# A masked softmax on one core: two whole loads move from SyncE's DMA queue to GpSimd's, ahead of the narrow loads

## The chip, the core and the metric

The kernel runs on one core of one Trainium2 chip. The metric is the device time in microseconds (us) of one execution; of the kernel before there are three, with a median of 155.32 us (155.14 to 155.57).

## The reference

The input is `x`, 16 batches x 8 heads x 256 rows x 256 columns in float32, and a length for each batch. In this draw the lengths lie between 157 and 252. Each row is a softmax over its first `length` columns; the columns behind are zero.

```python
for b in range(batch):
    length = lengths[b]
    masked = x[b, :, :, :length].copy()
    masked = masked - np.max(masked, axis=-1, keepdims=True)
    exp_masked = np.exp(masked)
    result[b, :, :, :length] = exp_masked / np.sum(exp_masked, axis=-1, keepdims=True)
```

## The kernel before

**Tiles.** One batch is one tile: 2,048 rows, 16 for each of 128 partitions, 256 columns, 2.1 MB. The buffer `xt` has eight slots for tiles; every step works in place. Tiles are taken in the order of `batch_of`: positions 0, 1 and 2 are batches 1, 2 and 3, position 3 is batch 0, and from position 4 on the position is the batch. In this text "tile 2" and "load 2" mean position 2.

**Loads.** The first three tiles are loaded whole, since they are fetched before the lengths are known. Tile 0 comes in two halves (L136), tiles 1 and 2 in one DMA each (L138), all issued by SyncE (SP), so they stand one behind the other in SP's queue, which the profile calls q1. From position 3 on GpSimd (POOL) issues *narrow* loads (`pick`, L158) through its own queue, q0: it reads the length into a register, walks through a tree of branches to the nearest width that is not smaller, and loads only so many columns of each row. (For lengths over the widest step it loads the whole tile.) The columns that such loads leave out are zeroed once for slots 3 to 7 (`fill`, L181).

**Compute, per tile.** VectorE (DVE) applies the mask (`clip`, L240: columns behind the length become hugely negative), ScalarE (ACT) does the exponential of 16 rows per partition and their sums in two halves (L347), and DVE takes reciprocals (L261) and multiplies (`divide`, L264), again in two halves. DVE's order is written out: the masks of tile 0's two halves, the divide of its first half, the mask of tile 1, the divide of its second half, then the mask of tile 2, both divides of tile 1, and from then on first divide, next mask, second divide.

**Stores.** SP issues them (L147) in two or three parts for most tiles, each after the divide that it needs (`s_out`). Ahead of all stores stands one wait for three masks (`s_min`, 3): both halves of tile 0 and tile 1. So stores share q1 with the first three loads, and come behind them.

**What orders POOL.** POOL makes constants (L171 to L177), waits for two early DVE steps, fills slot 3, and waits for the lengths, for its fill, and for the second half of tile 0 (`s_ld[1]`). Then come narrow load 3, the fills of slots 4 to 7, a wait for them and one for two divides (`s_out`, 2), and a loop (L193) for the remaining loads, in which load n waits until load n-2 has landed and the stores of the tile that had its slot are done:

```python
fill(ahead)
nc.gpsimd.wait_ge(s_word, 16)
nc.gpsimd.wait_ge(s_fill, 1)
nc.gpsimd.wait_ge(s_ld[1], 16)
v_len = length(POOL, word[0:1, 0:1])
pick(v_len, 0, ahead, 1, [160, 176, 192, 208, 224, seq_k])
for b in range(ahead + 1, slots):
    fill(b)
nc.gpsimd.wait_ge(s_fill, slots - ahead)
nc.gpsimd.wait_ge(s_out, 2)
```

At the end a check of all sums decides whether a slow exact path runs; it does not run with this data.

Of the kernel before, what the change touches and what calls it, by code (L numbers as in the profile page):

```python
# [21 lines left out]
def kernel(  # L22
# [6 lines left out]
    nc = tc.nc  # L29
# [9 lines left out]
    x_f = x.rearrange("b h q k -> b (h q) k").rearrange("b (p t) k -> b p t k", p=P)  # L39
# [5 lines left out]
    ahead = 3  # L45
    assert ahead == 3 and slots == 8 and batch == 16

    def batch_of(pos):
        return pos + 1 if pos < ahead else 0 if pos == ahead else pos
# [22 lines left out]
    xt = pool.tile([P, slots, nt, seq_k], F32, name="xt")  # L72
# [26 lines left out]
    with tc.tile_critical(no_gpsimd_drain=True):  # L99
# [4 lines left out]
        s_ld = [sem(f"s_ld{k}") for k in range(ahead + 1)]  # L104
# [8 lines left out]
        s_out = sem("s_out")  # L113
# [10 lines left out]
        def length(engine, at):  # L124

            return nc.values_load(
                at,
                engines=[engine],
                skip_runtime_bounds_check_because="compared with constants, never an address",
            )  # L130
# [3 lines left out]
        for h in range(2):  # L134
            s = slice(h * half, (h + 1) * half)
            nc.sync.dma_start(out=xt[:, 0, s], in_=x_f[batch_of(0), :, s]).then_inc(s_ld[h], 16)  # L136
        for b in range(1, ahead):
            nc.sync.dma_start(out=xt[:, b], in_=x_f[batch_of(b)]).then_inc(s_ld[b + 1], 16)  # L138

        nc.sync.wait_ge(s_min, 3)  # L140
        for b in range(batch):
            s_b = s_st[b % 2]
            for s in parts(b):
                nc.sync.wait_ge(s_out, 2 * b + (s.stop - 1) // half + 1)
                if b >= 2 and s.start == 0:
                    nc.sync.wait_ge(s_b, 64 * (b // 2 + 1))
                nc.sync.dma_start(  # L147
                    out=out_f[batch_of(b), :, s, :], in_=xt[:, b % slots, s, :]
# [26 lines left out]
        nc.gpsimd.memset(ones_c, 1.0).then_inc(s_ones, 1)  # L175
        for par in range(2):
            nc.gpsimd.memset(seed[:, par : par + 1], 0.0).then_inc(s_st[par], 64)  # L177
        nc.gpsimd.wait_ge(s_v, 2)

        def fill(b):  # L180
# [2 lines left out]
        fill(ahead)  # L183
        nc.gpsimd.wait_ge(s_word, 16)
        nc.gpsimd.wait_ge(s_fill, 1)
        nc.gpsimd.wait_ge(s_ld[1], 16)
        v_len = length(POOL, word[0:1, 0:1])
        pick(v_len, 0, ahead, 1, [160, 176, 192, 208, 224, seq_k])
        for b in range(ahead + 1, slots):
            fill(b)  # L190
        nc.gpsimd.wait_ge(s_fill, slots - ahead)
        nc.gpsimd.wait_ge(s_out, 2)
        with nc.Fori(0, batch // 2 - 2, 1, engines=[POOL]) as q:  # L193
            for par in range(2):
                n = 2 * q + (ahead + 1 + par)
# [19 lines left out]
        def step(ins):  # L215
# [8 lines left out]
                out=down, in0=iota_i, scalar1=0.5, scalar2=-big, op0=ALU.add, op1=ALU.mult  # L224
# [7 lines left out]
                out=len_s, in0=len_f, scalar1=big, scalar2=None, op0=ALU.mult  # L232
# [65 lines left out]
        for k, (_, _, edge, op) in enumerate(checks):  # L298
            nc.vector.tensor_scalar(  # L299
                out=bad[:, k : k + 1],  # L300
# [13 lines left out]
        with nc.vector.Else():  # L314
            with nc.Fori(0, batch, 1, engines=[DVE]) as i:
                nc.vector.wait_ge(g_ld, 16 * i + 16)
                nc.vector.scalar_tensor_tensor(
                    out=g_t,
# [8 lines left out]
                    out=neg_max, in_=g_t, op=ALU.max, axis=AX, negate=True  # L327
# [5 lines left out]
                    out=g_t,  # L333
# [25 lines left out]
        with nc.scalar.If(a_redo >= 1):  # L359
            for par in range(2):  # L360
                nc.scalar.wait_ge(s_st[par], 64 * (batch // 2 + 1))
            with nc.Fori(0, batch, 1, engines=[ACT]) as i:
                nc.scalar.dma_start(out=g_t, in_=x_g[:, bass.ds(i, 1)]).then_inc(g_ld, 16)
                nc.scalar.wait_ge(g_v, 3 * i + 2)
                with nc.Fori(0, nt, 1, engines=[ACT]) as t:
                    e = g_t[:, bass.ds(t, 1), :]
                    nc.scalar.activation(
                        out=e,
                        in_=e,
# [41 lines left out]
```

## Time and profile before

| | before |
|---|---|
| median of three executions | 155.32 us |
| the profiled execution | 155.53 us |
| its span, first to last instruction | 153.9 us |
| DVE busy | 116.9 us, 76% |
| ACT busy | 105.4 us, 68% |
| POOL busy | 21.6 us, 14% |
| bytes moved | 61.57 MB (read 27.98, written 33.55), mean 400 GB/s |

The profile is one execution. Its page gives busy time for each engine, then the span in 40 equal slices of 3.85 us; in the row of DMA each digit is the busy share of the 16 DMA engines in tenths, and the row below has what they moved. Queues are named by number: q1 is SP's, q0 is POOL's. Further views list an engine's instructions in order of time (start, duration, engine, line, operation, and in brackets the idle time before and what ended it), the chain of waits back from the last instruction, and busy time and GB/s in windows of one's choice. A DMA's landing is the time when its completion is seen; the trace also has a record of every DMA packet, with its queue, size and start. All times count from the start of the span.

### The profile page before, as it was taken

The numbers are of one execution on the slowest core, as the hardware profiler recorded it, in microseconds if no ns is written. First come the engines' busy times: TensorE is split into PE (matmuls) and PEld (weight loads), VectorE is DVE, ScalarE is ACT, GpSimd is POOL, SyncE is SP. The second block draws the span as 40 slices with busy tenths as digits, with TensorE's granted clock in tenths as the row PEclk, the third lists the DMA queues.
The fourth block names the chain that finished last, engine by engine and source line by source line (L and its number), as shares of the span: only waits on it lengthen the run. The fifth ranks groups of instructions, "written<-read, shape, count | busy, mean of one in ns | idle before, by whom it ended". The sixth has DMA issues, their size and how long they took to land.

```text
span 153.9 us, 1306 instructions
## 1 busy us (share of the span) xinstructions
PE 0.3 (0%) x2; PEld 0.2 (0%) x2; DVE 116.9 (76%) x91; ACT 105.4 (68%) x514; POOL 21.6 (14%) x28
## 2 busy tenths in 40 slices
PE   0000000000000000000000000000000000000000
PEld 0000000000000000000000000000000000000000
DVE  1359779997969696969889696969697676968700
ACT  3096899569595959597795959595968819597000
POOL 4139320100220200202030020211010000000000
DMA  4999999999999999999999999999999999999992
GB/s 124 428 445 419 319 376 418 414 409 442 416 404 387 423 411 420 409 414 415 400 421 411 413 411 404 411 420 415 418 416 421 424 441 417 430 449 413 432 422 119
DMA packets 10357, 61.57 MB, mean 400 GB/s; under 512 B 866, under 2 KB 978, under 8 KB 6642
## 3 DMA queue, kind: packets, MB, share of 16 engines
q1 hardware_dynamic: 5904, 39.85, 63.0%
q0 software_dynamic: 4448, 21.69, 35.2%
q14 instruction: 3, 0.02, 0.0%
q10 hardware_dynamic: 2, 0.00, 0.0%
HBM read 27.98 MB, written 33.55 MB: 400 GB/s over the span
## 4 chain that ended last, share of the span: by engine, by line
DMA 44%; DVE 29%; ACT 10%; issue 7%; ACTq 3%; SPq 1%; POOLq 0%; PE 0%
DMA xt<-in_x_dram 25%; DMA out_dram<-xt 19%; DVE xt L264 15%; DVE xt L240 12%; ACT xt L347 10%; ACTq L347 3%; DVE inv_sum L261 1%; SPq L136 1%; DVE ends L296 0%; SPq L147 0%; ACTq L353 0%; SPq L138 0%; DVE bad L299 0%; PE count L210 0%; POOLq L163 0%
## 5 line engine op out<-in xcount | busy, mean ns | idle before, releaser
L347 ACT ACTIVATE xt<-xt (+1 forms) x256 | 102.4, 402 | 34.3 <-DVE xt L240 34.3
L264 DVE TENSOR_TENSOR xt<-xt,inv_sum 128x2048 f32<-128x2048 f32 x32 | 73.3, 2292 | 1.1
L347 ACT ACTIVATION_READ_ACCUMULATOR xt<-xt (+1 forms) x256 | 48.0, 187 | 0.0
L240 DVE SCALAR_TENSOR_TENSOR xt<-down,len_s,xt 128x2048 f32<-128x2048 f32 (+1 forms) x17 | 37.8, 2221 | 8.2 <-DMA xt<-in_x_dram 8.1
L158 POOL DMA_DIRECT2D xt<-in_x_dram x13 | 13.9, 1073 | 90.4 <-DMA out_dram<-xt 60.1
L261 DVE RECIPROCAL inv_sum<-row_sum 128x8 f32<-128x8 f32 x32 | 6.4, 199 | 16.6 <-ACT xt L347 16.6
L181 POOL MEMSET xt<- 128x1536 f32 x5 | 6.7, 1400 | 1.1 <-DVE len_s L231 1.1
L340 ACT ACT_TABLE_LOAD x1 | 1.3, 1283 | 1.6 <-SPq L99 1.6
L223 DVE TENSOR_SCALAR down<-iota_i 128x256 f32<-128x256 int32 x1 | 0.3, 300 | 1.6 <-POOL iota_i L171 1.6
L296 DVE TENSOR_REDUCE ends<-row_sum 128x1 f32<-128x256 f32 x2 | 0.7, 410 | 0.0
L210 PE MATMUL count<-bad,ones_c 128*1 128x3 bf16 x1 | 0.2, 165 | 142.3 <-DVE bad L299 142.3
L228 DVE CAST len_b<-word 1x16 bf16<-1x16 int32 x1 | 0.2, 161 | 0.4 <-DMA word<-in_lengths_dram 0.4
L231 DVE TENSOR_SCALAR len_s<-len_f 128x16 f32<-128x16 f32 x1 | 0.2, 175 | 0.4 <-PE len_f L208 0.4
L171 POOL IOTA iota_i<- 128x256 int32 x1 | 0.3, 332 | 0.6 <-SPq L99 0.6
L307 DVE TENSOR_REDUCE redo<-count 1x1 f32<-1x3 f32 x1 | 0.1, 150 | 0.3 <-PE count L210 0.3
L299 DVE TENSOR_SCALAR bad<-ends 128x1 bf16<-128x1 f32 x3 | 0.3, 150 | 0.0
L177 POOL MEMSET seed<- 1x1 f32 x2 | 0.2, 226 | 0.0
L210 PEld LDWEIGHTS count<-bad,ones_c 128*1 128x1 bf16 x1 | 0.1, 79 | 142.4 <-DVE bad L299 142.4
L340 ACT ACTIVATE warm<-const-float32-0.0 128x1 f32<-128x1 f32 x1 | 0.2, 203 | 0.0
L174 POOL MEMSET ones<- 1x128 bf16 x1 | 0.2, 195 | 0.0
L208 PE MATMUL len_f<-len_b,ones 1*128 1x16 bf16 x1 | 0.2, 168 | 2.6 <-DVE len_b L228 2.6
L296 DVE TENSOR_REDUCE ends<-len_s 128x1 f32<-128x16 f32 x1 | 0.2, 159 | 0.0
(7 smaller groups left out, 0.6 us busy)
## 6 DMA issues: line engine op xcount, KB each, us to landing
out_dram<-xt SPq DMA_DIRECT2D x21, 1024.0 KB
out_dram<-xt SPq DMA_DIRECT2D x14, 512.0 KB
xt<-in_x_dram POOLq DMA_DIRECT2D x3, 1728.0 KB, 16.4
xt<-in_x_dram SPq DMA_DIRECT2D x2, 2048.0 KB, 14.4
xt<-in_x_dram POOLq DMA_DIRECT2D x2, 2048.0 KB, 15.7
out_dram<-xt SPq DMA_DIRECT2D x2, 2048.0 KB
xt<-in_x_dram POOLq DMA_DIRECT2D x2, 1600.0 KB, 15.9
xt<-in_x_dram POOLq DMA_DIRECT2D x2, 1280.0 KB, 14.2
```

The source lines that it names most:

```text
L136: nc.sync.dma_start(out=xt[:, 0, s], in_=x_f[batch_of(0), :, s]).then_inc(s_ld[h], 16)
L158: nc.gpsimd.dma_start(out=xt[:, slot, :, :w], in_=x_n[:, b, :, :w]).then_inc(s_sw[par], 16)
L171: nc.gpsimd.iota(iota_i, pattern=[[1, seq_k]], base=0, channel_multiplier=0).then_inc(s_iota, 1)
L181: nc.gpsimd.memset(xt[:, b, :, low:], 0.0).then_inc(s_fill, 1)
L210: nc.tensor.matmul(count, lhsT=ones_c, rhs=bad, start=True, stop=True).then_inc(s_count, 1)
L223: nc.vector.tensor_scalar(out=down, in0=iota_i, scalar1=0.5, scalar2=-big, op0=ALU.add, op1=ALU.mult)
L240: return nc.vector.scalar_tensor_tensor(out=t, in0=down[:, None, lo:hi].to_broadcast([P, s.stop - s.start, hi - lo]), scalar=len_s[:, batc ...
L261: step(nc.vector.reciprocal(out=inv_sum[:, b, s], in_=row_sum[:, b, s]))
L264: nc.vector.tensor_tensor(out=t, in0=t, in1=inv_sum[:, b, s, None].to_broadcast([P, half, seq_k]), op=ALU.mult,).then_inc(s_out, 1)
L296: step(nc.vector.tensor_reduce(out=ends[:, k : k + 1], in_=values, op=op, axis=AX))
L340: nc.scalar.activation(out=warm, in_=nc.const_aps.tensor(0.0, (P, 1), F32), func=EXP)
L347: ins = nc.scalar.activation(out=e, in_=e, func=EXP, accum_out=sum_h[:, i, j])
```

## The change

The loads of tiles 1 and 2 are issued by POOL, after its small constants and ahead of its first fill. They go through POOL's queue, and the narrow loads come behind them in the same queue. SP's queue is left with tile 0 and the stores; the wait for three masks ahead of the stores stays. Two of POOL's waits are dropped: that for the second half of tile 0 ahead of narrow load 3, and that for two divides ahead of the loop. No compute instruction is added, removed or moved on DVE, ACT or TensorE, and the bytes of every load and store are the same.

```diff
         for h in range(2):
             s = slice(h * half, (h + 1) * half)
             nc.sync.dma_start(out=xt[:, 0, s], in_=x_f[batch_of(0), :, s]).then_inc(s_ld[h], 16)
-        for b in range(1, ahead):
-            nc.sync.dma_start(out=xt[:, b], in_=x_f[batch_of(b)]).then_inc(s_ld[b + 1], 16)
-
         nc.sync.wait_ge(s_min, 3)
...
         for par in range(2):
             nc.gpsimd.memset(seed[:, par : par + 1], 0.0).then_inc(s_st[par], 64)
+        for b in range(1, ahead):
+            nc.gpsimd.dma_start(out=xt[:, b], in_=x_f[batch_of(b)]).then_inc(s_ld[b + 1], 16)
         nc.gpsimd.wait_ge(s_v, 2)
...
         nc.gpsimd.wait_ge(s_word, 16)
         nc.gpsimd.wait_ge(s_fill, 1)
-        nc.gpsimd.wait_ge(s_ld[1], 16)
         v_len = length(POOL, word[0:1, 0:1])
...
         nc.gpsimd.wait_ge(s_fill, slots - ahead)
-        nc.gpsimd.wait_ge(s_out, 2)
         with nc.Fori(0, batch // 2 - 2, 1, engines=[POOL]) as q:
```

## The prediction

> **What bounds the kernel now.** I read the page's row of DMA share first, then the same in unequal windows, then the queues, then GpSimd's (POOL's) timeline.
>
> ```profile
> DMA  4999999999999999999999999999999999999992
> GB/s 124 428 445 419 319 376 418 414 409 442 416 404 387 423 411 420 409 414 415 400 421 411 413 411 404 411 420 415 418 416 421 424 441 417 430 449 413 432 422 119
> q1 hardware_dynamic: 5904, 39.85, 63.0%
> q0 software_dynamic: 4448, 21.69, 35.2%
> ```
>
> The 16 DMA engines are busy from the second slice to the last but one, while DVE has 76% and ACT 68%. So the time is bytes over rate: 61.57 MB, which the change leaves alone, plus about 2 us before the first data and the last landing. One slice stands out, the fifth, with 319 GB/s. In windows (columns: window, length, then PE, PEld, DVE, ACT, POOL busy, clock, DMA share, GB/s):
>
> ```profile
> 4.00:8.00 4.00, 0.00 (x0) 0.00 (x0) 1.29 (x1) 0.54 (x3) 0.44 (x1) 1.00 1.04 438
> 8.00:12.00 4.00, 0.00 (x0) 0.00 (x0) 2.46 (x3) 4.00 (x21) 1.99 (x2) 1.00 1.03 438
> ...
> 15.00:16.70 1.70, 0.00 (x0) 0.00 (x0) 1.67 (x3) 0.65 (x3) 1.67 (x2) 1.00 0.96 403
> 16.70:20.40 3.70, 0.00 (x0) 0.00 (x0) 1.94 (x2) 3.70 (x20) 0.00 (x0) 1.00 1.00 281
> 20.40:24.00 3.60, 0.00 (x0) 0.00 (x0) 3.57 (x3) 3.54 (x19) 1.15 (x1) 1.00 1.01 415
> ```
>
> Whole loads alone run at 438 GB/s. For 3.7 us the engines are fully busy at 281 GB/s, which costs 3.7 x (1 - 281/415) = 1.2 us. In this stretch only reads are under way: the end of load 2 and narrow load 3 (loads counted by tile position, from 0). It ends when the first stores flow. They were issued at 15.82 (SP row of the timeline), but stood behind load 2 in SP's queue, and load 2 landed at 19.97 (issue 2.51, 17.46 us in the chain of waits). This stretch is what I price the change by.
>
> How two queues share, by the DMA view of two windows, 15 to 17 us and 36 to 41 us (packets, MB, share):
>
> ```profile
> q1 hardware_dynamic: 41, 0.67, 88.5%
> q0 software_dynamic: 43, 0.20, 24.2%
> ```
>
> ```profile
> q0 software_dynamic: 111, 1.79, 83.4%
> q1 hardware_dynamic: 108, 0.42, 20.5%
> ```
>
> The packets go one for one, whatever their size, so bytes divide as packet sizes do. A packet of a whole load is 16.4 KB (window 9 to 12: 79 packets, 1.29 MB), of the first tile's halves 8.2 KB (window 3 to 7: 213 packets, 1.61 MB, 16 of them the end marks). The Trainium skill (DMA: Bandwidth & Descriptors, "Queues, rings and completion order") says that each engine takes turns between queues packet by packet; the counts agree, 41 to 43.
>
> **The change, part by part.** *SP loses two issues* (L138, 2.05 to 3.19). SP then waits until 15.8 anyway: nothing gained.
>
> *POOL gains two issues* before its first fill. A whole load's issue on POOL is 0.56 us (the load of position 5, at 28.97), so loads 1 and 2 are issued from about 1.95 (end of the seeds) to 3.1. The timeline of POOL before:
>
> ```profile
> 1.70 0.25 POOL L177 MEMSET seed<- 1x1 f32 x2
> 3.06 1.39 POOL L181 MEMSET xt<- 128x1536 f32 x1 [1.10 <-DVE len_s L231]
> 10.01 1.30 POOL L158 DMA_DIRECT2D xt<-in_x_dram  x1 [5.57 <-issue]
> 11.31 5.36 POOL L181 MEMSET xt<- 128x1536 f32 x4
> 20.90 1.15 POOL L158 DMA_DIRECT2D xt<-in_x_dram  x1 [4.24 <-issue]
> ```
>
> The fill started at 3.06 and moves by 0.1 us; the issues lie in the 1.10 us of idle time.
>
> *The two waits that go.* Without the wait for tile 0 (landed 8.5: issue 1.58 + 6.9), narrow load 3 goes out at about 3.2 + 1.4 (fill) + 1.5 (8.5 to 10.01, length and branches) = 6.1. Without the wait for two divides, load 4 follows the four fills (6.1 + 1.3 + 5.4 = 12.8) by 2.7 (18.23, end of the second divide, to 20.90), at 15.5. Both queue behind loads 1 and 2 on the same queue, whose bytes last to 17.8 (below), so their earliness buys nothing; that cover would have to be gone by about 11 for it to count (6.1 plus 4.9, next paragraph).
>
> *The first tile loses its queue to itself.* This is the part that counts. When do POOL's first data flow? The trace has no whole load on an idle POOL queue. Lower bound: SP's first issue at 1.14 had its first packet at 2.15 (packet records), 1.0 us. Upper bound: narrow load 3, issued 10.01, first packet 14.95, 4.9 us. Load 6, also narrow, issued 38.10, had its first packet at 42.56, 4.5 us. A whole load's issue lasts 0.56 against 1.16 us of load 6, so I scale: 4.5 x 0.56/1.16 = 2.15, and take first data at 1.95 + 2.15 = 4.1, estimated. (The Trainium skill, same page, "Specifications", gives about 1 us for this path and 0.6 for the other; by that the data flow near 3 and the sum is the lower bound's, +1.3.)
>
> From then on tile 0 gets a third of 430, 143 GB/s. By 4.1 it has 0.55 MB (2 to 4 us: 254 GB/s). First half: 0.50 MB left, 3.5 us, landed with 0.4 for completion at 8.0 (6.0 before). Second half: 1.05 MB/143 = 7.3 us, to 14.9, landed 15.3 (8.5 before). DVE's order is fixed, mask of the second half ahead of divide and mask of tile 1: 15.35 + 1.3 (mask) = 16.65 (ACT has finished the first half by 12.7); + 2.53 (reciprocal and divide, 10.79 to 13.32) = 19.2; + 0.1 + 2.35 (mask of tile 1) = 21.65. The kept wait for three masks, at the head of SP's stores, opens there (15.79 before); all stores are behind it. Issue 21.7, first data 1.0 later: 22.7. Before, stores flowed from 20.4.
>
> Meanwhile the reads: 0.51 MB by 4, at 430 5.97 MB by 16.7; the last 0.32 MB of load 2 at 281 end at 17.8, and narrow load 3 (1.57 MB) feeds the queue to 23.4. So the queue stays full, but with reads only, until 22.7. If reads alone run at 281 from 16.7 on, as before, the slow stretch grows by 22.7 - 20.4 = 2.3 us, and 2.3 x (1 - 281/415) = **+0.74 us**.
>
> *After that nothing is late.* DVE starts the mask of tile 2 at 24.2 instead of 20.00. A tile of compute takes 8.38 us (divides at 35.76, 44.14, 52.52 in the chain), one of DMA 61.57/16 MB at 415 = 9.3 us, so the 4.2 us are made good in five tiles. Stores do not run dry: tile 0's 2.1 MB against narrow packets (4.6 KB; 64% of 415) last from 22.7 to 30.6, and tile 1's first half is divided by 29.0. At the end, stores alone run solid from 131 to 151 at 427 GB/s, the last 1 MB issued at 144.0 with some 4.5 us to spare.
>
> **Sum.** The profiled execution: span 153.9, time 155.53, which is 0.21 over the median of 155.32. 155.53 + 0.74 = 156.27; on the median, 156.06. I give 156.1. With the two bounds of the first data: at 3.0, tile 0 lands 1.8 us later still, +1.3; at 6.9, tile 0 lands at 9.7, the mask of tile 1 ends at 16.0, stores flow at 17.0, and 3.4 us of the slow stretch go, -1.1. Scaling places it nearer the first.
>
> **Rivals.** (1) *POOL's first data come late*: beyond 5.3 us (each us later brings tile 0's end, and the stores, 2 us forward; 22.7 must come to 20.4) the change gains, because stores no longer stand behind load 2. At 6.9, 154.2. For it: both rows of narrow loads, 4.5 and 4.9 us. Against: they make descriptors for 2,048 rows, a whole load for 128.
> (2) *The slow stretch is not reads alone*, but something of that place, such as load 2's rows beside narrow load 3's. For it: at 15 to 16.7 the same two loads ran at 403, and whole loads at 438. It would then be gone: -1.2, 154.1. Against: it outlives load 2 and ends just with the first stores.
> (3) *Any two queues of reads are slow together.* Then 281 GB/s hold from 4.1: 12.6 us to 16.7 x (1 - 281/430) = 4.4; tile 0 lands near 21, stores flow at 28, and 7.6 us x 0.32 = 2.4 come on top: 162, or 159 if it is half as deep. Against: 403 at 15 to 16.7.
> (4) *Nothing measurable*: first data near 5.3, or a slow stretch that ends with load 3's first rows. 155.3. The Trainium skill (same page, "Issuing engines are not separate DMA queues") says that spreading issues over engines saves only sequencer time, since all run on the same DMA engines: by that rule SP's 1.1 us of issue is all that is at stake and nobody waits for it. The full DMA row bears it out for bytes, not for the order of landing.
>
> **Chances.** Forecast 0.45 (own range 155.7 to 157.3), (1) 0.13, (2) 0.15, (3) 0.12, (4) 0.15. A measurement here tells 0.3%, 0.5 us, from no change. Faster 0.28, same 0.15, slower 0.57. The range takes in (1), (2) and (4) and the lower part of (3): 154.1 to 158.6; it leaves out what lies beyond on both sides, some 2 in 10.
>
> **What would show it.** Packets of POOL's queue from about 4 us, one for one with SP's; tile 0's second mask near 15.4, not 8.54; first store issue near 21.7, not 15.82; a slow window from near 17 to 23. Wrong if that window is at 415, if the first windows fall below 400, or if DVE waits for loads after 40 us or the last store is issued later than 148.

## The result, and the profile after

The changed kernel takes 155.80 us (median of 13 runs, 155.53 to 156.12) against 155.33 us of before (13 runs): a ratio of 1.0026, 95% interval 1.0016 to 1.0035, some 0.4 us. A second series of 12 runs gave 1.0014 (1.0003 to 1.0026), some 0.2 us. So it is slightly slower, on the side that was forecast and inside the stated range, by a little over half of the 0.74 us; it also lies within the 0.3% that the prediction counted as no change. The profiled execution took 156.12 us with a span of 154.4.

The page's rows of DMA and GB/s, after:

```profile
DMA  4999999999999999999999999999999999999991
GB/s 113 427 431 435 378 327 414 415 447 418 407 399 391 421 412 417 414 410 418 397 419 413 406 416 404 423 410 417 418 420 416 438 431 418 427 431 454 412 414 76
q1 hardware_dynamic: 5616, 35.65, 56.1%
q0 software_dynamic: 4736, 25.89, 41.9%
```

The two loads have changed queues (4.2 MB from q1 to q0). The weak place is still there in the fifth and sixth slices, but its lowest slice is now the sixth: 378 and 327 instead of 319 and 376. The windows of the prediction, after (DMA share and GB/s at the end of each line):

```profile
4.00:8.00 4.00, 0.00 (x0) 0.00 (x0) 1.28 (x1) 0.30 (x1) 2.62 (x3) 1.00 1.07 442
8.00:12.00 4.00, 0.00 (x0) 0.00 (x0) 0.00 (x0) 3.00 (x16) 4.00 (x4) 1.00 0.99 418
15.00:16.70 1.70, 0.00 (x0) 0.00 (x0) 1.70 (x2) 1.70 (x9) 0.83 (x1) 1.00 0.99 424
16.70:20.40 3.70, 0.00 (x0) 0.00 (x0) 3.67 (x3) 2.32 (x13) 0.00 (x0) 1.00 0.98 351
20.40:24.00 3.60, 0.00 (x0) 0.00 (x0) 3.57 (x4) 3.60 (x20) 0.00 (x0) 1.00 1.04 345
```

Look at the DVE column of 8 to 12: no work at all. DVE waits for tile 0's second half. The start on DVE, SP and POOL, from the timelines of after:

```profile
6.38 1.28 DVE L237 SCALAR_TENSOR_TENSOR xt<-down,len_s,xt 128x1024 f32<-128x1024 f32 x1 [3.27 <-DMA xt<-in_x_dram]
12.93 1.28 DVE L237 SCALAR_TENSOR_TENSOR xt<-down,len_s,xt 128x1024 f32<-128x1024 f32 x1 [5.27 <-DMA xt<-in_x_dram]
...
16.57 2.35 DVE L237 SCALAR_TENSOR_TENSOR xt<-down,len_s,xt 128x2048 f32<-128x2048 f32 x1
...
18.95 10.45 SPq L144 DMA_DIRECT2D out_dram<-xt  x5
...
1.94 1.21 POOL L176 DMA_DIRECT2D xt<-in_x_dram  x2
3.17 1.39 POOL L180 MEMSET xt<- 128x1536 f32 x1
5.94 1.17 POOL L155 DMA_DIRECT2D xt<-in_x_dram  x1 [1.38 <-issue]
7.11 5.36 POOL L180 MEMSET xt<- 128x1536 f32 x4
14.66 1.16 POOL L155 DMA_DIRECT2D xt<-in_x_dram  x1 [2.20 <-issue]
```

The mask of tile 0's second half moves from 8.54 to 12.93, and the first store's issue from 15.82 to 18.95. The sharing is as read from before: in the window 7 to 10 us of after the packets of the two queues go one for one, and the bytes two to one (packets, MB, share):

```profile
q0 software_dynamic: 52, 0.85, 69.0%
q1 hardware_dynamic: 49, 0.40, 32.2%
```

**Where the 0.4 us are.** Not in the weak stretch. 17 to 23 us run at 332 GB/s, which loses 6 x (1 - 332/415) = 1.2 us, and before lost 3.7 x (1 - 281/415) = 1.2 us too. The same window, before and then after:

```profile
17.00:23.00 6.00, 0.00 (x0) 0.00 (x0) 4.20 (x4) 5.93 (x30) 1.15 (x1) 1.00 0.95 323
17.00:23.00 6.00, 0.00 (x0) 0.00 (x0) 5.96 (x4) 4.62 (x23) 0.00 (x0) 1.00 0.99 332
```

By the packet records of loads and stores both kernels have moved 8.41 MB by 24 us, and 60.99 MB by 150 us. The difference is at the very end, in the last store's 16 completion marks. (A mark is the 4-byte packet that closes a DMA. Each DMA has 16 of them, and they are read here as one for each of the 16 DMA engines; the records do not name the engine.)

```
profiled execution     mean of 16 ends   last end   last behind the mean
before                      151.30        152.27        0.97
before, second profile      151.25        152.00        0.75
after                       151.31        152.74        1.43
after, second profile       151.28        152.55        1.27
```

The mean engine ends at the same time; the last one ends 0.5 us later. The first column is called the mean end below, the third the lag. The span ends some 1.6 us after the last mark in all fourteen profiles of this text, so what the last mark loses, the kernel loses.

### The profile page after: what moved, and what is told of

It reads as the page before. It is cut to its first block, busy times and chain, and to the rows that moved or that the text cites. A ratio compares the mean times of both kernels' runs of the same rounds, so it can differ in the third digit from the quotient of the medians.

```text
span 154.4 us, 1305 instructions
## 1 busy us (share of the span) xinstructions
PE 0.3 (0%) x2; PEld 0.2 (0%) x2; DVE 116.7 (76%) x91; ACT 105.4 (68%) x514; POOL 22.7 (15%) x30
## 4 chain that ended last, share of the span: by engine, by line
DVE 47%; ACT 21%; issue 12%; DMA 7%; ACTq 6%; SPq 0%; PE 0%
DVE xt L261 22%; DVE xt L237 21%; ACT xt L344 21%; DMA xt<-in_x_dram 7%; ACTq L344 5%; DVE inv_sum L258 2%; ACTq L350 1%; DVE ends L293 0%; SPq L136 0%; DVE bad L296 0%; PE count L207 0%; DVE redo L304 0%; SPq L403 0%; SPq L99 0%
## 5 line engine op out<-in xcount | busy, mean ns | idle before, releaser
L155 POOL DMA_DIRECT2D xt<-in_x_dram x13 | 13.8, 1063 | 89.7 <-DMA out_dram<-xt 65.6
L176 POOL DMA_DIRECT2D xt<-in_x_dram x2 | 1.2, 604 | 0.0
```

Source lines behind the costliest of these rows:

```text
L155: nc.gpsimd.dma_start(out=xt[:, slot, :, :w], in_=x_n[:, b, :, :w]).then_inc(s_sw[par], 16)
L176: nc.gpsimd.dma_start(out=xt[:, b], in_=x_f[batch_of(b)]).then_inc(s_ld[b + 1], 16)
```

## The experiments

The theories, as they came up. A: what counts is how long reads run alone, until the first stores' data flow. B: the totals are level, and the end is set by the one DMA engine that has fallen behind the others. C: the slow stretch is a fixed debt near the start. D: irregular slow packets come with the start of the first store. "Last end" below is that of the last store's completion marks, as in the table above.

### The changed kernel and the kernel before once more

No edit.

> The changed kernel once more, unchanged, for a second profile. Theory A (reads alone are slow: what counts is the time from about 17 us until the first stores' data flow) expects the window 17 to 23 us near 332 GB/s again. Theory B (the total is level by 150 us and the end is set by the one DMA engine that finishes last) expects the last completion some 1.4 us behind the mean of the 16 engines, as in the first profile (152.74 against 151.31), where before has 0.97 (152.27 against 151.30). If the straggler was chance, the lag here is near 1.0 and B falls. Time: 1.003 of before under both.

> The kernel before once more, unchanged, for a second profile. Theory B (changed and before are level in bytes and in the mean end of the 16 DMA engines, and differ in the last engine's lag) expects a lag of 0.9 to 1.1 us between the mean and the last engine's end (0.97 in the first profile; 1.43 and 1.27 in the two of the changed kernel). A lag of 1.3 or more would take that explanation away. The slow stretch should lie at 16.7 to 20.4 us near 281 GB/s again.

Measured: the lags are in the table above, 1.27 for after, 0.75 for before; the ratio of after was 1.0014, that of before against its fellows 0.9992 (0.9981 to 1.0004). B holds with two profiles of each. The slow stretch of before is there again, at 301 GB/s from 17.0 to 20.8.

### Stores without their first wait (e3)

```diff
-        nc.sync.wait_ge(s_min, 3)
```

> The changed kernel without the wait for three masks ahead of the stores: the first store is issued when the first divide ends, near 16.7 us instead of 18.95. Theory A: the slow stretch of reads ends 2.3 us sooner, and 2.3 x (1 - 332/415) = 0.46 us come back: 0.997 of the changed kernel, 1.000 of before. Theory B: the end stays with the last engine, 1.003 of before. Also: from issue to first data the first store took some 4 us in the changed kernel (18.95 to about 22.9); if that is the queue's own delay, its data flow here near 20.7; if it is the reads ahead of it in the engines, it may differ.

Measured: 1.001 (0.9998 to 1.0021), the same as the changed kernel's 1.0014 beside it. The first store was issued at 16.89 instead of 18.72 and its data flowed from 21.2 instead of 23.0. The 1.8 us gained nothing: 17 to 23 us ran at 336 GB/s, and the mean end was 151.37 (151.31 and 151.28 in the changed kernel), the last 152.52, lag 1.15. Theory A's 0.46 us did not come. (The interval alone reaches the 1.000 that A expected; the mean end decides.) The 336 is the mean of two unlike parts. Here is e3, then the changed kernel:

```profile
18.50:21.20 2.70, 0.00 (x0) 0.00 (x0) 2.67 (x3) 1.82 (x9) 0.00 (x0) 1.00 0.97 276
21.20:23.00 1.80, 0.00 (x0) 0.00 (x0) 1.80 (x2) 1.80 (x11) 0.00 (x0) 1.00 1.02 408
```

```profile
18.50:21.20 2.70, 0.00 (x0) 0.00 (x0) 2.67 (x3) 2.03 (x11) 0.00 (x0) 1.00 1.04 336
21.20:23.00 1.80, 0.00 (x0) 0.00 (x0) 1.80 (x2) 1.80 (x10) 0.00 (x0) 1.00 1.01 317
```

The early stores did end the slow stretch sooner, but ahead of their data the same reads, nearly all of them narrow, ran at 276 instead of 336 GB/s (328 in the changed kernel's second profile).

### The move alone, and the waits alone (e1, e2)

e1 puts POOL's two waits back into the changed kernel; e2 takes only them out of the kernel before.

```diff
+        nc.gpsimd.wait_ge(s_ld[1], 16)       # e1, ahead of narrow load 3
...
+        nc.gpsimd.wait_ge(s_out, 2)          # e1, ahead of the loop
```

> Only the move of loads 1 and 2; POOL's two waits are kept. Narrow load 3 is then issued near 14.4 (landing of tile 0 at 12.9 + 1.5), its first data some 4.5 to 4.9 us later near 19, and load 2 ends near 17.5: a hole of about 1.5 us without any traffic, unless stores fill it (first data near 23). Theory A: slower than the changed kernel by that hole, +1.5 us, less what the shorter stretch of narrow reads gives back: 1.006 to 1.010 of before. Theory B: as far as the hole is on all engines alike it comes on top too: 1.010 or more. My forecast that the earliness of the narrow loads buys nothing would say 1.003.

> Only POOL's two waits go; loads 1 and 2 stay in SP's queue. Narrow load 3 is issued near 6 and flows from about 11, one packet for one with loads 1 and 2, which land later: tile 1 at about 13.8, load 2 at about 21.5. Theory A: reads are then alone until load 2 is through SP's queue, about 21 instead of 20.4, so +0.2 us: 1.001 of before. Theory B: no sharing with tile 0, engines as close as before: 1.000.

Measured: e1 1.0054 (1.0037 to 1.0071), e2 1.0000 (0.9987 to 1.0013). The move alone costs two to four times as much as the whole change (1.0026 and 1.0014), and the dropped waits alone give nothing. The hole of e1 is not where I had put it (narrow load 3 still came at 17.6, as load 2 ended). The last packet of load 3 comes at 24.26; load 4 goes out at 24.21, and its first packet comes at 27.35. Meanwhile the stores flow alone and run dry: their data stop at 28.2 and go on at 29.25. DMA share and GB/s of e1, then of after:

```profile
24.00:27.00 3.00, 0.00 (x0) 0.00 (x0) 2.97 (x3) 3.00 (x16) 1.43 (x2) 1.00 1.01 427
27.00:29.00 2.00, 0.00 (x0) 0.00 (x0) 1.60 (x2) 2.00 (x12) 0.29 (x1) 1.00 1.00 282
29.00:31.00 2.00, 0.00 (x0) 0.00 (x0) 1.97 (x2) 2.00 (x12) 0.00 (x0) 1.00 0.99 354
```

```profile
27.00:29.00 2.00, 0.00 (x0) 0.00 (x0) 1.61 (x2) 2.00 (x11) 0.00 (x0) 1.00 1.00 409
29.00:31.00 2.00, 0.00 (x0) 0.00 (x0) 1.97 (x2) 2.00 (x11) 0.00 (x0) 1.00 1.01 416
```

2 x (409 - 282)/415 + 2 x (416 - 354)/415 = 0.9 us, which is most of the 1.0 us by which the mean end is later than after (152.30 against 151.31). By 40 us e1 is 0.4 MB behind, and stays so to the end.

### Stores later (e7)

```diff
-        nc.sync.wait_ge(s_min, 3)
+        nc.sync.wait_ge(s_min, 4)
```

> The changed kernel with stores that wait for a fourth mask (that of tile 2): first issue near 23.6 us instead of 18.9, first data near 27.6. Theory A (the loss grows with the time for which reads run alone at 332 instead of 415 GB/s): 4.7 x 0.2 = 0.9 us more than the changed kernel, 1.008 of before. Theory C (the loss is a fixed debt of some 0.5 MB near the start, since five kernels so far have moved 8.36 to 8.42 MB by 24 us whatever their order): the bytes by 30 us and the time stay, 1.002 of before.

Measured: 1.0040 (1.0025 to 1.0056). First store issued at 23.07, data at 26.7, 3.6 us after those of the changed kernel; the mean end is 0.35 later (151.66). So C falls, since the loss does grow, but with half of A's price. Narrow reads run alone for 8 us and do so steadily:

```profile
18.50:22.50 4.00, 0.00 (x0) 0.00 (x0) 4.00 (x2) 3.91 (x19) 0.00 (x0) 1.00 1.04 331
22.50:26.50 4.00, 0.00 (x0) 0.00 (x0) 3.93 (x5) 4.00 (x22) 0.56 (x1) 1.00 1.01 336
```

### Load 3 whole (e8)

```diff
-        pick(v_len, 0, ahead, 1, [160, 176, 192, 208, 224, seq_k])
+        pick(v_len, 0, ahead, 1, [seq_k])
```

> The changed kernel with load 3 whole (2.10 MB in 128 rows of 16 KB) instead of narrow (1.57 MB in 2,048 rows of 768 bytes); 0.52 MB more are read, 1.25 us at 420 GB/s. If the slow stretch belongs to narrow rows that are read with no stores beside them, the window 17 to 23 us shows some 430 GB/s and the slow stretch moves behind load 3 or goes: time of the changed kernel or up to +0.3 us. If any reads alone are slow after 17 us (theory A as a rate, or a fixed debt, C): near 332 in that window as before, and +1.25 us, 1.010 of before.

Measured: 1.0063 (1.0045 to 1.0081); the mean end is 152.20, 0.9 us after that of the changed kernel for 1.25 us' worth of bytes. The windows split the slow stretch in two kinds:

```profile
18.00:20.40 2.40, 0.00 (x0) 0.00 (x0) 2.37 (x3) 1.60 (x8) 0.00 (x0) 1.00 1.01 423
20.40:23.00 2.60, 0.00 (x0) 0.00 (x0) 2.60 (x2) 2.60 (x15) 0.00 (x0) 1.00 1.02 274
```

Whole reads alone run at 423 until 20.4, where the narrow reads of the changed kernel were already at 331. Then whole reads too drop to 274, though no narrow packet has come yet (the first at 24.05), and recover when the first store's data flow, at 22.9. That store was issued at 18.58. Hence theory D, which e3 fits as well. The changed kernel does not fit it: its first store was issued at 18.95, and the reads stayed at 336 and 317 until the data came.

### All loads on POOL's queue (e6)

Tile 0's two halves are issued by POOL ahead of loads 1 and 2.

```diff
-            nc.sync.dma_start(out=xt[:, 0, s], in_=x_f[batch_of(0), :, s]).then_inc(s_ld[h], 16)
+            nc.gpsimd.dma_start(out=xt[:, 0, s], in_=x_f[batch_of(0), :, s]).then_inc(s_ld[h], 16)
```

> Tile 0's halves too are issued by POOL, ahead of loads 1 and 2: one queue for all loads, tile 0 has it to itself, and POOL's first data flow with nothing else under way. If the 4 us from issue to first data (1.94 to 5.95 in the changed kernel) are the software queue's own, data begin near 6 instead of 2.2: +3.8 us, 1.025 of before. If they come from the busy engines, data begin near 3 to 3.5: +1 us, 1.007. Theory B (engines drift apart while two queues share tile 0's time) expects the last engine no later than in before against the mean, near 1.0 us.

Measured: 1.0096 (1.0079 to 1.0112), more than the 1.007 expected; data begin 1.2 us later than in before (3.33 against 2.15), and the mean end, 152.53, is 1.2 later too. Issued at 1.94, first packet at 3.33: 1.4 us on idle engines, where the same queue took 4.0 (1.94 to 5.95) beside SP's loads. So the late first data of the changed kernel are not POOL's own delay. The lag is 1.03, as B had it for a kernel without sharing. SP's queue is empty here until the first store, issued 17.29; its data still come only at 21.4.

### Only load 2 moved (e9)

```diff
+        nc.sync.dma_start(out=xt[:, 1], in_=x_f[batch_of(1)]).then_inc(s_ld[2], 16)
         nc.sync.wait_ge(s_min, 3)
...
-        for b in range(1, ahead):
+        for b in range(2, ahead):
             nc.gpsimd.dma_start(out=xt[:, b], in_=x_f[batch_of(b)]).then_inc(s_ld[b + 1], 16)
```

> Only load 2 is moved to POOL's queue, without POOL's two waits; load 1 stays on SP behind tile 0. Load 2 then shares from about 6 us, with two thirds against tile 0's second half and one half against load 1, so tile 1 lands near 17 and the stores issue near 19 to 20: no better than the changed kernel. Theory A and C both: 1.001 to 1.003 of before. Theory B: less sharing with tile 0, 1.001.

Measured: 1.0051 (1.0036 to 1.0065), worse than I had it. Load 1 now stands behind a tile 0 that gets a third of the rate, and its last packets flow near 19; the first store is issued at 22.75, its data come at 26.4. As in e7 the mean end is late (151.70). The lag is 1.39, and theory B's 1.001 did not come either. B had counted on less sharing with tile 0, but load 2's first packet came at 6.1 and tile 0's last at 11.6, as those of load 1 and tile 0 in the changed kernel, so the sharing was as long.

### The kernel before with early stores, and with a later narrow load (e12, e11)

e12 drops the wait for three masks from the kernel before. e11 keeps it, but in the kernel before fills all five slots first and holds narrow load 3 until load 1 has landed, right ahead of its issue; the wait for two divides goes.

```diff
-        nc.sync.wait_ge(s_min, 3)             # e12
...
+                if isinstance(b, int):        # e11, in pick, ahead of the DMA
+                    nc.gpsimd.wait_ge(s_ld[2], 16)
```

> The kernel before without the wait for three masks ahead of the stores: the first store is issued near 13.3 instead of 15.8 us and stands in the queue behind load 2 for longer. Theory A (reads alone, until stores flow): nothing changes, stores still flow when load 2 is through, slow from about 16.7 to 20.4, 1.000 of before. Theory D (the irregular slow packets come with the start of the first store: in before they begin 0.9 us after its issue, in the kernel with load 3 whole 1.9 us after it): the slow stretch begins 2.5 us sooner, near 14.2, and either ends sooner (faster by up to 0.5 us) or only grows (slower).

> The kernel before with narrow load 3 held until load 1 has landed (13.4 us) instead of tile 0 (8.5), its length read and all five fills done ahead of that wait, and without the wait for two divides. Issued near 13.6, it flows near 18, when load 2 is nearly through and stores are at hand. Theory A: load 2 is whole and alone, so 430 GB/s to 17.9, and from then stores and narrow reads together at 415: the slow stretch goes, -1.2 us, 0.992 of before. Theory D: the slow packets come with the first store's start, whatever is read: 280 to 330 GB/s from 16.7 to about 19.5 stay, 0.998 to 1.000.

Measured: e12 1.0013 (1.0003 to 1.0022), e11 1.0046 (1.0030 to 1.0061). e12 first: 424 GB/s from 13.0 to 15.5, then 303 to 19.5. Its store was issued at 13.60, 2.2 us before that of before (15.82), and the slow stretch begins about 1 us sooner and is no shorter: D's sign, with half its size; A had expected no change. e11 was to be the better kernel, with 0.992 by A and 0.998 to 1.000 by D, and is not:

```profile
13.00:17.40 4.40, 0.00 (x0) 0.00 (x0) 4.26 (x4) 2.32 (x13) 2.27 (x2) 1.00 1.00 424
17.40:21.40 4.00, 0.00 (x0) 0.00 (x0) 3.85 (x4) 4.00 (x21) 0.17 (x1) 1.00 0.91 258
21.40:24.00 2.60, 0.00 (x0) 0.00 (x0) 2.57 (x3) 2.60 (x14) 0.00 (x0) 1.00 1.02 413
```

Load 2 had left SP's queue at 18.3, and the first store, issued at 16.23, was next in it, but its data came at 21.1. So in the kernel before, too, the stores were not held up by load 2 alone: 15.82 plus some 4.4 us is 20.3, when they flowed.

### Loads 1 and 2 on ScalarE's queue (e5)

```diff
+        for b in range(1, ahead):
+            nc.scalar.dma_start(out=xt[:, b], in_=x_f[batch_of(b)]).then_inc(s_ld[b + 1], 16)
...
-            nc.gpsimd.dma_start(out=xt[:, b], in_=x_f[batch_of(b)]).then_inc(s_ld[b + 1], 16)
```

> The changed kernel with loads 1 and 2 issued by ScalarE (a hardware queue, as SP's) right after the lengths, near 1.6 us, instead of by POOL. If the first data of a queue come late because the engines are busy, they come here after 1.0 to 1.4 us as on idle engines, near 2.7, since the engines are hardly busy yet. By packets one for one tile 0 then gets a third from the start: its second half lands near 16.5 to 17, the mask of tile 1 ends near 23, first store data near 27 with the 4 us that the stores took so far: slower than the changed kernel by the 4 us of reads alone, +0.4 to +0.8 us (the later stores of the fourth mask cost 0.35), 1.005 to 1.008 of before. If instead order does not matter: 1.002.

Measured: 1.0032 (1.0021 to 1.0042), less than the 1.005 to 1.008 expected for late stores. Issued at 1.66, first packet at 5.68: 4.0 us on a hardware queue, as on POOL's, and not the 1.0 to 1.4 that I expected. The first store was issued at 20.35, its data came at 24.3; mean end 151.47, lag 1.41.

No kernel of these beats the kernel before; e2 is level with it.

## Why the prediction was right, and where it was not

**The sign and the chain of events were right, the term that made the sum was not.** The forecast 0.74 us came from the slow stretch, which measured 0.0; the 0.4 us came from the last mark, which stood at nothing in the sum. That the time came out near the forecast is luck. Step by step:

- *What SP and POOL issue.* 1.21 us for two issues from 1.94, fill at 3.17, narrow load 3 at 5.94 (forecast 6.1), load 4 at 14.66 (15.5). Right.
- *"Their earliness buys nothing."* Wrong. It covers a slow stretch near 28 us, worth 0.9 us, in which the stores run dry while load 4 is late; e1 shows it. With the waits kept the change would have cost 1.0054.
- *POOL's first data, estimated at 4.1 by scaling.* They came at 5.95. The scaling by the length of the issue had no basis: e6 shows 1.4 us on idle engines, e5 4.0 us for a hardware queue on busy ones. The row that it should have been nearest to was the other one, 4.5 to 4.9 us. So tile 0 lost less than forecast: second mask at 12.93, not 15.35, first store issued at 18.95, not 21.7.
- *First store data 1.0 us after issue, 22.7.* They came at 23.1, but 4.2 us after the issue. Two errors of opposite sign, each above 2 us, left the forecast time of the stores nearly exact; the range does not owe that to insight. Bound by the wrong row again: SP's first load started on idle engines.
- *The slow stretch grows by 2.3 us at 281 GB/s, +0.74 us.* This term failed. The stretch did last to 23 us, but at 332 instead of 281, and measured 0.0: 8.41 MB by 24 us in both kernels. The 281 of before is not the rate of reads alone: narrow reads alone held 331 to 336 for 8 us in e7, and e3 fell to 276 where the changed kernel had 336, with an edit that moves only the stores. e3 ended the stretch sooner by 1.8 us and gained nothing; e7 ended it 3.6 us later and lost 0.35.
- *"After that nothing is late."* True of the bytes (60.99 MB by 150 us) and of the mean engine; not of the last one. The measured 0.4 us fit the lag of the last DMA engine, 1.43 and 1.27 against 0.97 and 0.75, which no term of the sum had.
- *The rivals.* (1) was near the truth in its premise (5.95, beyond my 5.3) and wrong in its gain, since the stores' own start took 4 us. (2) is wrong in its time, since the stretch did not go, but half right in its premise: the depth of 281 belonged to that place, and 332 came instead. (3) falls: the two queues of reads ran at 442 and 418 GB/s. (4) was the nearest for the bytes. The rule of the Trainium skill that was weighed there (DMA: Bandwidth & Descriptors, "Issuing engines are not separate DMA queues") agrees with the level totals; the order of landing moved all the same, by 4.4 us for tile 0.

**What stays open.** Why one engine falls further behind is not settled. The nine profiles with loads moved out of SP's queue have lags of 1.03 to 1.43, the five with these loads on SP 0.66 to 1.04. In both profiles of after one engine ends load 2 at 18.8 us, some 0.7 us after all the others, beside an 8 KB instruction fetch at 16.96 and 16.99; but e2 has such a fetch at 17.22 and a lag of 0.66, so the fetch alone is not the cause. It is not needed either: e1's first such fetch comes at 26.46, its last mark of load 2 is only 0.2 us behind the next, and its lag is 1.19. Part of the lag arises late. Over the last 20 us, in which stores run alone, it grows by 0.21 to 0.27 us in all nine, and not at all in four of the five; but the first profile of before grows by 0.22 too.

Nor is it settled what makes reads drop below the rate of narrow reads alone just ahead of the first store's data. In eight profiles the first store was issued while a whole load had packets to come for another 1.4 us or more (before, twice; e2, e3, e6, e8, e11, e12); in the last 1.5 us ahead of its data these ran at 230 to 298 GB/s. In the other six the last whole packet started before that issue or at most 0.3 us after it (after, twice; e1, e5, e7, e9), and they ran at 327 to 349. That the two go together is seen, not explained.

## What to carry to other kernels

Where the DMA engines are full throughout, moving a transfer to another queue changes who lands first, not the total; look for its price at the last engine's end and at the places where a queue may run dry, not in the mean rate. A queue that joins busy engines should be priced from a row in which another queue was busy too, never from the first DMA of the kernel. The mean rate of a window can hide two unlike parts: e3's 336 was 276 and 408. And when a time comes out right, check each step: here two wrong steps cancelled.

## What the runs showed of the hardware

- From issue to first packet: 1.0 us (SP) and 1.4 us (POOL) on idle engines; 4.0 us (POOL's whole load), 4.0 (ScalarE's queue) and 3.5 to 4.9 (SP's first store, in thirteen profiles; 6.0 in e12, where it stood behind load 2) beside another queue's traffic. The Trainium skill (DMA: Bandwidth & Descriptors, "Specifications") gives a first-byte latency of about 1 us for POOL's path and 0.6 for SP's; the idle rows are of that order, the busy ones are not.
- Narrow reads with no other traffic run at 331 to 336 GB/s for 8 us (e7); a 4.6 KB packet then takes 229 to 236 ns (nine in ten of them), and 178 beside stores in before. Whole reads alone run at 423 to 442, except just ahead of the first store's data (274 in e8).
- The 16 completion marks of the last store come up to 2.2 us apart (150.6 to 152.7 in after), and the kernel's time goes by the last.
